# A hybrid SSD decoder block on one Trainium2 core: normalising y inside the SSD steps, and forming block sums of w_down beside the MLP

## The chip, the cores and the metric

The kernel runs on one core of one Trainium2 chip. The metric is the device time of one execution in microseconds; the time of a kernel is the median of its runs. Five engines work in order, each on its own list of instructions: TensorE (PE, with its weight loads shown as PEld), VectorE (DVE), ScalarE (ACT), GpSimd (POOL) and SyncE (SP, which here only issues DMAs; ACT issues some too).

## What is computed

One decoder layer over 1024 positions, width 1024, all in float32, cut to what matters here:

```python
u = rmsnorm(h, norm_mix_w)
gate_a, gate_s, b_a, c_a, v_a, z, xbc, dt_raw = split(u @ w_in)
y_a = (b_a * causal_dwconv3(c_a * v_a)) @ w_a_out
xs, bs, cs = split(silu(causal_dwconv4(xbc) + ssd_conv_b))
y = ssd_chunked_scan(xs, dt, a, bs, cs) + d_skip * xs       # 4 groups, 8 chunks of 128 positions
yf = y * silu(z)                                            # per group of 512 channels:
yf = yf * rsqrt(mean(yf * yf over the group) + 1e-5)        # one factor per position and group
y_s = (yf * ssd_norm_w) @ w_s_out
h = h + (sigmoid(gate_a) * y_a + sigmoid(gate_s) * y_s) @ w_o
v = rmsnorm(h, norm_ffn_w)
h = h + (silu(causal_dwconv3(v @ w_1) + b) * (v @ w_3)) @ w_down
out = rmsnorm(h, final_norm_w)
```

## The kernel before

Every large product is done in three matmuls on a high and a low part of each operand (`split`: ACT casts the high part, DVE or POOL subtracts it to give the low part), 128 rows of weights by 512 positions at a time. Twelve such matmuls, a `product`, are the unit in which the kernel counts: each call of `product` for a `Pair` of output tiles ends in a `tick()`. Pairs of output tiles share sums of blocks (a Strassen-like scheme; the products are named b11, b21, t1 to t4 and b22), so a pair takes seven products.

The stages follow one another on PE. First u is normalised and transposed, then come the projections of w_in with the SSD beside them. The SSD is 32 chunk steps (4 groups, 8 chunks each; `ssd_chunk`), written as a generator with eight parts. The part that runs is set by a table of ticks: step s starts around tick 17 + 6 s, and `STAGES` gives the offset of each part (loading the decay table, loading the chunk, decays, transposes, loading z, the diagonal blocks and the state, squares, norm). Then come the y_a product (`y_a`, two halves of 512 positions), the product with w_s_out (`s_out`, two halves), the product with w_o (`out_proj`), the MLP's 22 up pairs (`ffn_pair`, finished by `ffn_done`), and four sweeps of the down product, which read the block sums of w_down from `td` in device memory and those of the gated activations from `s3d`, `s21d` and `s4d`.

The order on each engine is set by a scheduler that plays the program through with its own durations, and by a few priorities; on the chip each engine then works through its list in that order.

At the end of a chunk step, `zt` holds y * silu(z) for 512 channels (four tiles of 128 channels on the partitions) by 128 positions. Before the change it is squared, summed over the four tiles by DVE into `ss`, and summed over the partitions by a matmul against a column of ones (`pn`, L813). DVE scales that (`yss`, L815), POOL takes the power -1/2 (`yr`, L819, 128 factors on 128 partitions), and `zt` itself is stored without the factor to `yd` (L807, issued by ACT). After four chunks the four columns of factors are transposed by PE (`pr`, L823), copied by ACT (`rr`, L825) and stored to `rd` (L826, SP). In `y_half`, beside `y_a`, each group's 512 factors are loaded back, broadcast to all partitions (`rb`), and DVE multiplies y by the channel's weight and `rb` (L926) before y is split.

The block sums of w_down are formed by `w_sums` (L869): two loads of 128x1024, four subtractions (two on DVE, two on POOL) and four stores to `td`, for each of 11 blocks. They run beside the first `s_out` and the second `y_a`, through `beside(...)`.

Of the kernel before, what the change touches and what calls it, by code (L numbers as in the profile page):

```python
# [8 lines left out]
F32 = mybir.dt.float32  # L9
F32R = mybir.dt.float32r  # L10
AF = mybir.ActivationFunctionType
ALU = mybir.AluOpType
# [41 lines left out]
STAGES = LOAD_M, LOAD_IN, DECAY, TRANS, LOAD_Z, DIAG, SQUARES, NORM = -9, -9, -6, -4, -3, 0, 3, 6  # L54
# [11 lines left out]
def tile_block(  # L66
# [340 lines left out]
    yd, rd = {}, {}  # L407
    for g in range(NG):
        for hf in range(2):
            yd[g, hf] = dram.tile([P, 4, HALF], F32, name=f"yd{g}{hf}")  # L410
            rd[g, hf] = dram.tile([HALF], F32, name=f"rd{g}{hf}")
# [288 lines left out]
    states, decayed, stats = {}, {}, {}  # L700

    def ssd_chunk(s):
# [104 lines left out]
        act.dma_start(yd[g, c // 4][:, :, hts], zt)  # L807
# [6 lines left out]
        rs = tiny(f"yss{nm}")  # L814
        dve.tensor_scalar(rs, pn, 1.0 / HALF, EPS, op0=ALU.mult, op1=ALU.add)  # L815
        if c % 4 == 0:
            stats[g, c // 4] = tiny(f"yr{nm}", 4)
        r = stats[g, c // 4]
        pool.tensor_tensor(r[:, c % 4 : c % 4 + 1], rs, nhalf, op=ALU.pow)  # L819
        if c % 4 == 3:  # L820

            pr = sd_tile(f"pr{nm}")[:4, :P]
            pe.transpose(pr, r, ident)  # L823
            rr = ssp.tile([P, P], F32, tag="ss", name=f"rr{nm}", bufs=1)
            act.copy(rr[:4, :], pr)  # L825
            sp.dma_start(rd[g, c // 4].rearrange("(c p) -> c p", c=4), rr[:4, :])  # L826
# [42 lines left out]
    def w_sums(k):  # L869

        r, r2 = (s4(f"wd{f}{k}")[:, :SEQ] for f in range(2))
        for f, t in enumerate((r, r2)):
            sp.dma_start(t, w_down[f * KF + k])
        b11, b12 = (r[:, h] for h in halves)
        b21, b22 = (r2[:, h] for h in halves)
        sub(b11, b12, b11)
        sub(b12, b22, b12, pool)
        sub(b22, b22, b11)
        sub(b21, b22, b21, pool)
        for i, t in enumerate((b11, b22, b12, b21)):  # L880
            sp.dma_start(td[k, i], t)

# [28 lines left out]
    def y_half(hf, res):  # L911
        for g in range(NG):
            rb = c2(f"rb{hf}{g}")
            sp.dma_start(
                rb,
                rd[g, hf].unsqueeze(0).to_broadcast([P, HALF]),
            )
            hi, lo = big_tile(f"yh{hf}{g}", F32R), big_tile(f"yl{hf}{g}", F32R)
            res.append((hi, lo))
            yt = (extra_tile if hf else big_tile)(f"y{hf}{g}")  # L920
            sp.dma_start(yt, yd[g, hf])
            for j in range(0, 4, 2):
                raw = yt[:, j : j + 2, :]
                for i in range(2):
                    w = wns[:, 4 * g + j + i : 4 * g + j + i + 1]
                    dve.scalar_tensor_tensor(  # L926
                        raw[:, i, :], raw[:, i, :], w, rb, op0=ALU.mult, op1=ALU.mult
                    )
                split(raw, hi[:, j : j + 2, :], lo[:, j : j + 2, :], dve)
                yield  # L930
# [81 lines left out]
    def all_sums():  # L1012
        for k in range(KF):
            w_sums(k)
            yield

# [4 lines left out]
    sums = all_sums()  # L1021
# [5 lines left out]
    mg0 = s_out(0, ys0, beside(ta_half(1, ta1), sums))  # L1027
    yh = y_half(1, ys1)
    y_a(1, ta1, beside(yh, yh, sums))
# [75 lines left out]
    def g_sums(i, cv, free):  # L1105

        a, b = (cv[:, h] for h in halves)
        if i < KF:
            s3 = free[:, :HALF]
            sub(s3, a, b)  # L1110
            sp.dma_start(s3d[i], s3)
            return
# [10 lines left out]
    def ffn_done(i):  # L1123
# [4 lines left out]
        dve.tensor_tensor(cv, cv, h3, op=ALU.mult)  # L1128
        sp.dma_start(gd[i], cv)
        g_sums(i, cv, h3)  # L1130
# [227 lines left out]
```

## Time and profile before

| | |
|---|---|
| median of 3 runs | 1973.02 us (1971.64 to 1974.24) |
| the profiled execution | 1974.46 us |
| its span, first to last instruction | 1972.7 us |
| mean granted TensorE clock | 0.989 |
| busy: PE, DVE, POOL, ACT | 97%, 65%, 63%, 49% |
| projections with the SSD beside them | about 100 to 954 us of the span |
| y_a, s_out and out_proj | about 954 to 1320 us |
| the MLP's up pairs | about 1320 to 1750 us |

A row of the profile names the line, the engine, the operation, the tile written and the tiles read, with numbers left out of the names; a count behind an x says how many instructions a row stands for. The idle time before an instruction is put down to what ended it. PE's busy time is a union of modelled intervals: consecutive matmuls overlap in it, so the distance from one start to the next is the price of a matmul, not the duration printed with it.

### The profile page before, as it was taken

The page shows a single profiled execution, that of the slowest core. Times are in us where ns is not written, and L with a number is a line of the kernel's source. Part 1 is how long each engine was busy: PE and PEld are TensorE (multiplying, and loading weights), DVE is VectorE, ACT ScalarE, POOL GpSimd, SP SyncE. Part 2 cuts the span into 40 slices and gives each one's busy share as a digit, 9 for nine tenths or more (in the row PEclk, how much of TensorE's full clock was granted, in tenths as well). Part 3 has the DMA queues.
Part 4 walks back from the last instruction along what each step waited for, and adds up shares of the span by engine and source line. Part 5 has one row for each costly group of instructions (what it writes and reads, how often), then busy time and mean ns, then how long its engine had stood idle before and what let it go on. Part 6 is the DMA issues. An engine that isn't in the chain of part 4 may idle for free.

```text
span 1972.7 us, 25409 instructions
## 1 busy us (share of the span) xinstructions
PE 1914.5 (97%) x8986; PEld 1572.0 (80%) x8986; DVE 1289.6 (65%) x1429; ACT 962.0 (49%) x1636; POOL 1236.3 (63%) x915
## 2 busy tenths in 40 slices
PE   7899999999999999999999999998999999999998
PEld 6678887787788778888888888876888888878886
DVE  8655567767776777777664833479854655585555
ACT  6345457677546664443542323354344444453334
POOL 6657776866776776676445533458876787845342
PEclk9899999999999999999999999998999999999999
DMA  4133355545445554443998974451323344487653
GB/s 166 54 111 121 122 164 172 162 150 190 155 133 164 164 164 124 146 157 110 382 376 279 356 250 161 161 170 35 136 80 108 101 150 163 139 285 264 206 188 143
DMA packets 180175, 338.42 MB, mean 172 GB/s; under 512 B 15280, under 2 KB 87760, under 8 KB 179024
## 3 DMA queue, kind: packets, MB, share of 16 engines
q1 hardware_dynamic: 93264, 253.95, 37.7%
q10 hardware_dynamic: 86784, 82.85, 13.1%
q8 instruction: 70, 1.15, 0.2%
q14 instruction: 57, 0.47, 0.1%
HBM read 247.34 MB, written 89.41 MB: 171 GB/s over the span
## 4 chain that ended last, share of the span: by engine, by line
PE 80%; DVE 7%; ACT 4%; issue 3%; DMA 3%; POOL 2%; ACTq 1%; SPq 0%; POOLq 0%; DVEq 0%
PE pb11up L268 10%; PE so L268 9%; PE pt1up L268 6%; PE pb11xb L268 5%; PE ya L268 4%; PE pb11cv L268 4%; PE d L1151 3%; PE d L1153 3%; PE d L1152 3%; PE pb11z L268 3%; PE pb21up L268 3%; PE pb11ba L268 2%; PE pt1cv L268 2%; PE pt1xb L268 2%; DMA m<-acd 2%
## 5 line engine op out<-in xcount | busy, mean ns | idle before, releaser
L608 DVE SCALAR_TENSOR_TENSOR cv<-xbc,scw,cv 128x1024 f32<-128x1024 f32 x72 | 122.6, 1704 | 46.3 <-ACT cv L604 45.0
L608 DVE SCALAR_TENSOR_TENSOR h<-fci,fcw,h 128x1024 f32<-128x1024 f32 x44 | 85.9, 1953 | 74.1 <-ACT h L604 73.3
L724 ACT ACTIVATE m<-m,tk 128x128 f32<-128x128 f32 x256 | 79.1, 390 | 95.3 <-DMA m<-acd 91.4
L149 POOL TENSOR_TENSOR l_ws<-raw_ws,h_ws 128x512 fp32r<-128x512 f32 x32 | 46.3, 1447 | 71.1 <-PE so L268 40.8
L148 ACT CAST h_ws<-raw_ws 128x512 fp32r<-128x512 f32 x64 | 39.9, 623 | 96.8 <-PE so L268 69.3
L268 PE MATMUL so<-yh,h_ws 128*128 128x512 f32 x256 | 69.0, 391 | 0.0
L268 PE MATMUL so<-yl,h_ws 128*128 128x512 f32 x256 | 68.6, 389 | 0.0
L268 PE MATMUL so<-yh,l_ws 128*128 128x512 f32 x256 | 68.5, 389 | 0.0
L148 ACT CAST h_wo<-raw_wo 128x512 fp32r<-128x512 f32 x48 | 29.7, 621 | 60.3 <-PE wo L985 32.7
L808 DVE TENSOR_TENSOR eb<-eb 128x256 f32<-128x256 f32 x32 | 28.1, 879 | 45.6 <-ACT eb L806 45.6
L149 DVE TENSOR_TENSOR l_ws<-raw_ws,h_ws 128x512 fp32r<-128x512 f32 x32 | 25.1, 785 | 50.0 <-PE so L268 25.5
L149 POOL TENSOR_TENSOR l_wo<-raw_wo,h_wo 128x512 fp32r<-128x512 f32 x24 | 32.3, 1346 | 39.1 <-PE wo L985 30.7
L268 PEld LDWEIGHTS so<-yh,l_ws 128*128 128x128 f32 x256 | 48.0, 188 | 10.0
L268 PEld LDWEIGHTS so<-yl,h_ws 128*128 128x128 f32 x256 | 48.0, 188 | 10.0
L268 PEld LDWEIGHTS so<-yh,h_ws 128*128 128x128 f32 x256 | 47.8, 188 | 9.7
L1128 DVE TENSOR_TENSOR h<-h 128x1024 f32<-128x1024 f32 x22 | 48.7, 2212 | 9.8 <-ACT h L1127 9.6
L314 DVE TENSOR_TENSOR fci<-fci,pb21up 128x512 f32<-128x512 f32 x18 | 12.4, 688 | 60.3 <-PE pb21up L268 60.3
L149 POOL TENSOR_TENSOR l_t3up<-raw_2up,h_t3up 128x512 fp32r<-128x512 f32 x22 | 30.3, 1376 | 32.7 <-PE pb11up L268 32.7
L984 PE MATMUL wo<-l_wo,mh 128*128 128x512 f32 x128 | 50.0, 391 | 0.0
L983 PE MATMUL wo<-h_wo,mh 128*128 128x512 f32 x128 | 49.9, 391 | 0.0
L985 PE MATMUL wo<-h_wo,ml 128*128 128x512 f32 x128 | 49.7, 391 | 0.0
L1127 ACT ACTIVATE h<-h 128x1024 f32<-128x1024 f32 x22 | 23.4, 1062 | 52.7 <-DVE h L608 52.7
(1125 smaller groups left out, 6571.8 us busy)
## 6 DMA issues: line engine op xcount, KB each, us to landing
m<-acd ACTq DMA_DIRECT2D x32, 512.0 KB, 3.9
raw_ws<-in_w_s_out SPq DMA_DIRECT2D x32, 512.0 KB, 4.7
ssd_in<-cv ACTq DMA_DIRECT2D x24, 512.0 KB, 3.1
in<-ssd_in ACTq DMA_DIRECT2D x32, 384.0 KB, 3.8
raw_wo<-in_w_o SPq DMA_DIRECT2D x24, 512.0 KB, 3.8
wd<-in_w_down SPq DMA_DIRECT2D x22, 512.0 KB, 7.0
td<-wd SPq DMA_DIRECT2D x44, 256.0 KB, 4.3
raw_2up<-in_w_up SPq DMA_DIRECT2D x22, 512.0 KB, 3.4
```

Source lines behind the costliest of these rows:

```text
L148: act.copy(hi, v)
L149: (eng or pool).tensor_tensor(lo, v, f32(hi), op=ALU.subtract)
L268: pe.matmul(ps, wt[:, k, :], ct[:, k, :], start=(start and n == 0), stop=(stop and n == 11), skip_group_check=held,)
L608: dve.scalar_tensor_tensor(cv, ci[:, j : j + SEQ], w[:, j : j + 1], cv, op0=ALU.mult, op1=ALU.add)
L724: act.activation(m[:, h, :], m[:, h, :], AF.Relu, bias=a)
L983: pe.matmul(pss[t], mh, wh, start=k == 0, stop=False)
L984: pe.matmul(pss[t], mh, wl, start=False, stop=False)
L985: pe.matmul(pss[t], ml, wh, start=False, stop=k == NK - 1)
L1128: dve.tensor_tensor(cv, cv, h3, op=ALU.mult)
L1151: pe.matmul(ps, aa[0][:, ts], bb[0], start=k == 0, stop=False)
L1152: pe.matmul(ps, aa[0][:, ts], bb[1], start=False, stop=False)
L1153: pe.matmul(ps, aa[1][:, ts], bb[0], start=False, stop=k == KF - 1)
```

## The change

Two things are moved. First, the factor of each chunk is applied to `zt` inside its own SSD step, before it is stored. POOL's power gives 128 factors on 128 partitions; DVE multiplies the identity by them into the tile of the sums, and a matmul of the 128x128 matrix of ones with that diagonal matrix puts the same 128 factors, along the positions, on every partition (`pr`). DVE then does the four multiplications by weight and factor (a `scalar_tensor_tensor` of 128x128 each, with `pr` read from PSUM) and ACT issues the store of the scaled `zt`. This is a ninth part of the step, SCALE, two ticks behind NORM; NORM moves from tick 6 to 5 and the load of z from -3 to -2. The transposes, the copies, the `rd` stores, the `rb` loads and the 32 multiplications in `y_half` go.

Second, `w_sums` is called from `g_sums`, for each of the MLP's first 11 pairs, once that pair's gated product is issued. Its two tiles are those of `side` (two buffers), and all four subtractions are DVE's.

```diff
-STAGES = LOAD_M, LOAD_IN, DECAY, TRANS, LOAD_Z, DIAG, SQUARES, NORM = -9, -9, -6, -4, -3, 0, 3, 6
+STAGES = LOAD_M, LOAD_IN, DECAY, TRANS, LOAD_Z, DIAG, SQUARES, NORM, SCALE = -9, -9, -6, -4, -2, 0, 3, 5, 7
...
         act.activation(sq, zt.rearrange("p j l -> p (j l)"), AF.Square)
-        act.dma_start(yd[g, c // 4][:, :, hts], zt)
...
         pe.matmul(pn, sums, ones[:, :1], start=True, stop=True)
-        rs = tiny(f"yss{nm}")
-        dve.tensor_scalar(rs, pn, 1.0 / HALF, EPS, op0=ALU.mult, op1=ALU.add)
-        if c % 4 == 0:
-            stats[g, c // 4] = tiny(f"yr{nm}", 4)
-        r = stats[g, c // 4]
-        pool.tensor_tensor(r[:, c % 4 : c % 4 + 1], rs, nhalf, op=ALU.pow)
-        if c % 4 == 3:
-
-            pr = sd_tile(f"pr{nm}")[:4, :P]
-            pe.transpose(pr, r, ident)
-            rr = ssp.tile([P, P], F32, tag="ss", name=f"rr{nm}", bufs=1)
-            act.copy(rr[:4, :], pr)
-            sp.dma_start(rd[g, c // 4].rearrange("(c p) -> c p", c=4), rr[:4, :])
+        r = tiny(f"yr{nm}")
+        dve.tensor_scalar(r, pn, 1.0 / HALF, EPS, op0=ALU.mult, op1=ALU.add)
+        pool.tensor_tensor(r, r, nhalf, op=ALU.pow)
+
+        dve.tensor_scalar(sums, ident, r, None, op0=ALU.mult)
+        yield
+        pr = sd_tile(f"pr{nm}")[:, :P]
+        pe.matmul(pr, ones, sums, start=True, stop=True)
+        for j in range(4):
+            w = wns[:, 4 * g + j : 4 * g + j + 1]
+            dve.scalar_tensor_tensor(zt[:, j, :], zt[:, j, :], w, pr, op0=ALU.mult, op1=ALU.mult)
+        act.dma_start(yd[g, c // 4][:, :, hts], zt)
...
     def y_half(hf, res):
-            rb = c2(f"rb{hf}{g}")
-            sp.dma_start(
-                rb,
-                rd[g, hf].unsqueeze(0).to_broadcast([P, HALF]),
-            )
...
-                for i in range(2):
-                    w = wns[:, 4 * g + j + i : 4 * g + j + i + 1]
-                    dve.scalar_tensor_tensor(
-                        raw[:, i, :], raw[:, i, :], w, rb, op0=ALU.mult, op1=ALU.mult
-                    )
                 split(raw, hi[:, j : j + 2, :], lo[:, j : j + 2, :], dve)
...
-    mg0 = s_out(0, ys0, beside(ta_half(1, ta1), sums))
+    mg0 = s_out(0, ys0, beside(ta_half(1, ta1)))
-    y_a(1, ta1, beside(yh, yh, sums))
+    y_a(1, ta1, beside(yh, yh))
...
+    def w_sums(k):
+
+        r, r2 = (side(f"wd{f}{k}", w_down[f * KF + k]) for f in range(2))
+        b11, b12 = (r[:, h] for h in halves)
+        b21, b22 = (r2[:, h] for h in halves)
+        sub(b11, b12, b11)
+        sub(b12, b22, b12)
+        sub(b22, b22, b11)
+        sub(b21, b22, b21)
+        for i, t in enumerate((b11, b22, b12, b21)):
+            sp.dma_start(td[k, i], t)
+
+    def g_sums(i, cv, free, after):
         a, b = (cv[:, h] for h in halves)
         if i < KF:
+            with tc.issue_after(after.ins):
+                w_sums(i)
             s3 = free[:, :HALF]
...
-        dve.tensor_tensor(cv, cv, h3, op=ALU.mult)
+        gated_ = dve.tensor_tensor(cv, cv, h3, op=ALU.mult)
         sp.dma_start(gd[i], cv)
-        g_sums(i, cv, h3)
+        g_sums(i, cv, h3, gated_)
```

The scheduler lays the new work into the engines' lists. In the rows below the number at the end of a tile's name only tells instances apart; `zt_2` is chunk 2 of its group.

DVE in the SSD stage, third group, chunks 2 and 3, before: the scaling of the sums (L815) stands between a pair's addition and the next chunk's diagonal.

```order
L810 TENSOR_TENSOR ss_2_5847<-eb_2_5652 128x128
L363 TENSOR_TENSOR z_5566<-u2z_5662,pt1z_5711 128x512
L815 TENSOR_SCALAR yss_2_5919<-pn_2_5917 128x1
L784 TENSOR_TENSOR in_3_5659<-in_3_5659,pd_3_5922 128x512
L786 TENSOR_TENSOR eb_3_5849<-po_3_5931,eb_3_5849 128x512
L787 TENSOR_TENSOR in_3_5659<-in_3_5659,eb_3_5849 128x512
L793 TENSOR_TENSOR st_5362<-sn_2_5753,pst_3_5936 128x512
L803 TENSOR_TENSOR zt_3_5852<-in_3_5659,zt_3_5852 128x512
```

The same place now: the product with the identity (L816) stands three instructions behind the scaling of the sums, and the four multiplications by `pr` (L822) behind the next chunk's `zt`.

```order
L813 TENSOR_SCALAR yr_2_5994<-pn_2_5992 128x1
L363 TENSOR_TENSOR z_5645<-u2z_5742,pt1z_5802 128x512
L149 TENSOR_TENSOR l_b22xb_6248<-raw_2xb_5946,h_b22xb_6247 128x512
L783 TENSOR_TENSOR in_3_5739<-in_3_5739,pd_3_6015 128x512
L816 TENSOR_SCALAR ss_2_5939<-ident,yr_2_5994 128x128
L785 TENSOR_TENSOR eb_3_5969<-po_3_6024,eb_3_5969 128x512
L786 TENSOR_TENSOR in_3_5739<-in_3_5739,eb_3_5969 128x512
L792 TENSOR_TENSOR st_5435<-sn_2_5839,pst_3_6029 128x512
L802 TENSOR_TENSOR zt_3_5972<-in_3_5739,zt_3_5972 128x512
L149 TENSOR_TENSOR l_t1g_6287<-raw_1g_6116,h_t1g_6286 128x512
L822 SCALAR_TENSOR_TENSOR zt_2_5762<-zt_2_5762,wns,pr_2_6069 128x128 x4
```

So L816, which needs POOL's power, now has the next chunk's L785 to L802 queued behind it.

PE at the same place, before: the sums over the partitions (`pn`) and then only the next chunk's matmuls and products.

```order
L813 MATMUL pn_2_5917<-ones,ss_2_5847 128x1
L770 MATMUL pd_3_5922<-m_3_5657,xd_3_5816 64x128 x8
L777 MATMUL po_3_5931<-in_3_5659,st_5362 128x128 x4
L783 MATMUL pst_3_5936<-xe_3_5818,bk_3_5821 128x512
L268 MATMUL pt1xb_5959<-us1h,h_t1xb_5960 128x512 x4
L268 MATMUL pt1xb_5959<-us1l,h_t1xb_5960 128x512 x4
L268 MATMUL pt1xb_5959<-us1h,l_t1xb_5961 128x512 x4
```

Now, behind `pn` and some two products:

```order
L268 MATMUL pt1xb_6052<-us1h,l_t1xb_6054 128x512 x3
L268 MATMUL pb11xb_5883<-us3h,h_t3xb_6077 128x512 x4
L268 MATMUL pb11xb_5883<-us3l,h_t3xb_6077 128x512 x4
L268 MATMUL pb11xb_5883<-us3h,l_t3xb_6078 128x512 x4
L268 MATMUL pb11g_6118<-ua11h,h_b11g_6119 128x512 x2
L819 MATMUL pr_2_6069<-ss_2_5939,ones 128x128
L729 MATMUL px_4_6093<-ident,in_4_5943 128x128 x4
```

A matmul that needs the power now follows `pn` in every chunk, 32 in all, where 8 transposes stood.

SP in the MLP, around one pair, before: the loads of two weight tiles, and two stores.

```order
L158 DMA raw_1up_12652<-in_w_up 128x1024
L1129 DMA gd<-h_12221 128x1024
L158 DMA raw_2up_12691<-in_w_up 128x1024
L1111 DMA s3d<-h_12221 128x512
L158 DMA raw_1up_12796<-in_w_up 128x1024
```

Now, from one pair's first weight tile to the next pair's:

```order
L158 DMA raw_1up_12712<-in_w_up 128x1024
L1110 DMA gd<-h_12245 128x1024
L1082 DMA td<-wd_12504 128x512
L158 DMA raw_2up_12751<-in_w_up 128x1024
L1092 DMA s3d<-h_12245 128x512
L1082 DMA td<-wd_12504 128x512
L1082 DMA td<-wd_12506 128x512 x2
L1069 DMA wd_12660<-in_w_down 128x1024
L1069 DMA wd_12662<-in_w_down 128x1024
L158 DMA raw_1up_12868<-in_w_up 128x1024
```

Each of the first 11 pairs has six more DMAs in SP's list, four of which wait for DVE, ahead of the next pair's first weight tile.

More of the change, by code (lines that the diff above doesn't have):

```diff
@@ L406, in tile_block @@
     acd = dram.tile([2, P, P], F32, name="acd")
-    yd, rd = {}, {}
+    yd = {}
     for g in range(NG):
@@ L410, in tile_block @@
             yd[g, hf] = dram.tile([P, 4, HALF], F32, name=f"yd{g}{hf}")
-            rd[g, hf] = dram.tile([HALF], F32, name=f"rd{g}{hf}")
     ead = dram.tile([2, P, P], F32, name="ead")
@@ L698, in tiles @@
         return t.rearrange("p (j l) -> p j l", j=4)
-    states, decayed, stats = {}, {}, {}
+    states, decayed = {}, {}
     def ssd_chunk(s):
@@ L867, in add @@
         eng.tensor_tensor(o, p, q, op=ALU.add)
[L869 to L881, printed above, removed]
     def ta_half(hf, res):
@@ L1010, in v_norm @@
         return v
[L1012 to L1015, printed above, removed]
     def beside(*gens):
         return lambda j: [next(g, None) for g in gens]
-    sums = all_sums()
     ta0, ta1, ys0, ys1 = [], [], [], []
@@ L1103, in side @@
         return t
-    def g_sums(i, cv, free):
+    def w_sums(k):
[9 more added lines that the diff above has]
+    def g_sums(i, cv, free, after):
         a, b = (cv[:, h] for h in halves)
         if i < KF:
+            with tc.issue_after(after.ins):
+                w_sums(i)
             s3 = free[:, :HALF]
```

## Prediction

> **What bounds the kernel now.** First the page's busy times and its chain of waits, then the engines by stretches (span, PE busy, PEld, DVE, ACT, POOL, granted clock, DMA share, GB/s).
>
> ```profile
> PE 1914.5 (97%) x8986; PEld 1572.0 (80%) x8986; DVE 1289.6 (65%) x1429; ACT 962.0 (49%) x1636; POOL 1236.3 (63%) x915
> PE 80%; DVE 7%; ACT 4%; issue 3%; DMA 3%; POOL 2%; ACTq 1%; SPq 0%; POOLq 0%; DVEq 0%
> ...
> 250.00:850.00 600.00, 587.59 (x3057) 478.62 (x3056) 442.89 (x523) 363.34 (x678) 422.86 (x322) 1.00 0.50 158
> 930.00:1000.00 70.00, 70.00 (x311) 57.81 (x310) 48.77 (x54) 32.67 (x47) 33.58 (x22) 1.00 0.95 361
> 1000.00:1100.00 100.00, 100.00 (x442) 82.68 (x441) 59.35 (x68) 35.07 (x53) 48.16 (x34) 1.00 0.90 319
> 1380.00:1400.00 20.00, 20.00 (x90) 16.41 (x89) 16.91 (x15) 7.23 (x12) 18.76 (x14) 1.00 0.53 175
> 1400.00:1420.00 20.00, 20.00 (x90) 16.57 (x89) 17.75 (x15) 8.15 (x13) 17.84 (x13) 1.00 0.22 76
> 1420.00:1500.00 80.00, 80.00 (x355) 66.24 (x354) 44.21 (x41) 35.63 (x56) 56.03 (x43) 1.00 0.31 101
> ```
>
> PE is the bound nearly everywhere: 58.2 us of the span (1972.7 - 1914.5) are all the time in which it has nothing to do. In the SSD stretch it idles 12.4 us of 600. From 930 to 1100, where the change takes work away, it idles not at all, although the DMA engines there are 90 to 95% busy. That "busy" could hide a slower cadence, so I read the cadence, from the chain in order of time (start, length, what) in that stretch and from PE's timeline in the MLP, where DMA is light; between them stands DVE's scaling of y by `rb` (ns least, median and most; first and last start).
>
> ```profile
> 1003.12 87.04 PE so L268 x384
> ...
> L926 DVE SCALAR_TENSOR_TENSOR y<-y,wns,rb x32: 737/745/1781, 966.8 to 1114.4; 128x512 f32<-128x512 f32 x32
> ...
> 1436.25 1.07 PE L268 MATMUL pt1up<-vs4h,l_b22up 128*128 128x512 f32 x4
> 1437.15 1.07 PE L268 MATMUL pt1up<-vs1h,h_t1up 128*128 128x512 f32 x4
> ```
>
> 87.04 / 384 = 227 ns a matmul, and (1437.15 - 1436.25) / 4 = 225 ns. The crowded stretch runs no slower. So whatever DVE, POOL, SP and the DMA engines get rid of between 930 and 1160 is worth nothing: the 32 multiplications of y by `rb` (median 745 ns), the 8 `rb` loads, and the 44 subtractions and 66 transfers of `w_sums`. What the change adds to PE, and every wait it makes for PE, does count.
>
> **PE's own work.** The timeline around two places of the SSD stage gives prices as distances between starts.
>
> ```profile
> 425.63 0.27 PE L732 MATMUL pb<-ident,in 128*128 128x128 f32 x1
> 425.74 0.39 PE L734 MATMUL pc<-in 128*128 128x128 f32 x2
> 425.88 1.17 PE L268 MATMUL pt1xb<-us1h,h_t1xb 128*128 128x512 f32 x4
> 426.89 1.08 PE L268 MATMUL pt1xb<-us1l,h_t1xb 128*128 128x512 f32 x4
> ...
> 436.88 0.28 PE L813 MATMUL pn<-ones,ss 128*128 128x1 f32 x2
> 437.02 1.18 PE L268 MATMUL pb11xb<-ua22h,h_t4xb 128*128 128x512 f32 x4
> 438.04 1.08 PE L268 MATMUL pb11xb<-ua22l,h_t4xb 128*128 128x512 f32 x4
> ...
> 937.51 0.27 PE L823 MATMUL pr<-ident,yr 128*4 128x128 f32 x1
> 937.53 1.17 PE L268 MATMUL pb21g<-ua12h,h_b21g 128*128 128x512 f32 x4
> 938.54 1.08 PE L268 MATMUL pb21g<-ua12l,h_b21g 128*128 128x512 f32 x4
> ```
>
> Four product matmuls take 0.91 us from start to start. `pc`, a float32 matmul of 128x128 by 128 columns like the new `pr`, has two records; from its start to the second group after it are 1.15 us, so it costs 0.24 us. `pn` comes to 0.25 by the same step, the transpose of the old `pr` to 0.12. New: 32 x 0.24 = 7.7 us. Gone: 8 x 0.12 = 1.0. Net +6.7 us, bounded below by 32 x 2 x 0.11 - 1.0 = 6.0 (each record priced as `pb`, 425.74 - 425.63) and above by 32 x 0.25 - 1.0 = 7.0. The Trainium skill's page "TensorE: Matmul & The Clock Gate" (Back-to-back issue gap) gives about 81 ns for a sustained matmul of 128 columns: two of these would make `pr` 0.16 us, 5.2 us in all, and an estimate of +4.2 net. Its 131 ns for 512 columns is not what this trace shows (225 ns), so I keep the rows' price.
>
> **Waits for the factor.** Before, the power was waited for by one transpose in four chunks. PE's waits, POOL's wait for DVE, and the slowest and the quickest of the 32 chunks (timeline):
>
> ```profile
> PE pr L823 <- POOL yr L819: 2.8, 3, 2.3
> POOL yr L819 <- DVE yss L815: 14.7, 8, 4.5
> ...
> 662.63 0.28 PE L813 MATMUL pn<-ones,ss 128*128 128x1 f32 x2
> 663.44 0.15 DVE L815 TENSOR_SCALAR yss<-pn 128x1 f32<-128x1 f32 x1
> 671.72 1.48 POOL L149 TENSOR_TENSOR l_t2g<-t2g,h_t2g 128x512 fp32r<-128x512 f32 x1
> 673.16 0.59 POOL L819 TENSOR_TENSOR yr<-yss,nhalf 128x1 f32<-128x1 f32 x1
> ...
> 751.36 0.28 PE L813 MATMUL pn<-ones,ss 128*128 128x1 f32 x2
> 752.00 0.55 POOL L819 TENSOR_TENSOR yr<-yss,nhalf 128x1 f32<-128x1 f32 x1
> ```
>
> POOL waited for DVE in only 8 chunks; in the other 24 POOL was the late one. From `pn`'s start to the power's end are 1.2 us at best and 11.1 at worst. The new `pr` stands about two products behind `pn` on PE, some 6.4 to 12.6 us of matmuls at the prices above, mostly 7.5 to 9.7. Set against each chunk's own delay, plus 0.35 us for DVE's multiplication of the identity, six chunks come late, three by 1.7 to 1.9 us, the others by less, 6.6 us in all. The 2.8 us of old waits go. The new ones could be 0 (POOL's list is new too) or 11.2 (all 32 wait the 0.35 us that the old eight averaged); I take 6.6.
>
> **DVE and ACT in the SSD stage.** DVE gets four multiplications and the identity's per chunk. The nearest row is a 128x128 operation that reads PSUM:
>
> ```profile
> L751 DVE TENSOR_TENSOR cb<-pc,tri 128x128 f32<-128x128 f32 x32 | 8.9, 278 | 0.0
> ACT m L724 <- DMA m<-acd: 84.9, 23, 6.9
> ```
>
> 5 x 0.28 = 1.4 us a chunk, 45 us in all. DVE goes from 443 busy of 600 to about 482. The worse part is that the identity's multiplication holds DVE's list until POOL is done: directly behind L813 in 13 chunks, one to three instructions later in the rest. Taking each chunk's old delay from DVE's scaling to the end of the power, less what stands between, I get about 80 us of standing, on top of 482 in 600; it largely replaces idle time. Queued behind it are the next chunk's `eb`, `st` and `zt`. Who waits for these: POOL's `sn`, ACT's squares, and PE through PSUM banks. The pairs are covered, as two rows of a product's low part and its use show for the MLP, and as I find for the SSD's pairs too (mostly 10 to 20 us):
>
> ```profile
> 1423.29 0.68 DVE L149 TENSOR_TENSOR l_b22up<-raw_2up,h_b22up 128x512 fp32r<-128x512 f32 x1
> ```
>
> It ends at 1423.97 and PE reads it at 1436.25, 12.3 us later. ACT's list now holds the `yd` store until DVE has scaled, and the copies that free PE's accumulators (u2, u3) stand behind it; ACT already loses 84.9 us there to the loads of `m`. For all of this I take +2 us. The ends are -12.4 (all of PE's idle time there vanishes by the new order) and +20 (a quarter of the 80 us reaches PE); I stay near zero because the rows show long leads.
>
> **The MLP.** 11 pairs get four subtractions on DVE. Their rows, and the transfers (KB each, us to landing):
>
> ```profile
> L864 DVE TENSOR_TENSOR wd<-wd x11: 678/693/1779, 931.6 to 1150.6; 128x512 f32<-128x512 f32 x11
> L864 POOL TENSOR_TENSOR wd<-wd,wd x11: 1284/1292/2379, 940.3 to 1153.7; 128x512 f32<-128x512 f32 x11
> td<-wd SPq DMA_DIRECT2D x44, 256.0 KB, 4.3
> wd<-in_w_down SPq DMA_DIRECT2D x22, 512.0 KB, 7.0
> ```
>
> 4 x 0.69 = 2.8 us a pair against 8.5 us of DVE idle time per pair of 19.1 us (7 products of 12 matmuls) from 1420 on (35.8 in 80): hidden, by idle DVE. The first four pairs are different, with shorter turns and DVE 85 to 89% busy from 1380 to 1420: 11 us of subtractions into 5.3 us of idle time. Pair 1's first subtraction also waits for a load that waits for pair 0's last store, 4.3 + 7.0 us by rows taken under crowded DMA. So DVE runs some 6 to 10 us late there, within the 12 us lead. On SP the next weights stand behind stores that wait for DVE, with about a pair's lead (19 us). I take +1; the ends are 0 and +10 (the lead is gone at the start).
>
> **The sum.** 6.7 - 2.8 + 6.6 + 2 + 1 = +13.5 us. The profiled execution took 1974.46 us, 1.8 beyond its span and 1.4 above the median of 1973.02. It would take 1988.0; from the median I forecast 1986.5 us. By the page's price for `pr` alone it would be 1984.0.
>
> **Rivals.**
> 1. POOL is not late in the new order and everything else is covered: +6.7 - 2.8 = +3.9, 1976.9 us, just at the edge of what a measurement of this kernel tells from no change (0.2%, 3.9 us). For it: 19 of the 32 old delays are under 5.5 us. Against it: POOL's list still has the same eight operations ahead of the late power at 662. If in addition PE's other idle time shrinks a little, the result is "same".
> 2. DVE's standing behind POOL becomes a bound: 482 + 75 of 600 us leave little to catch up; a quarter reaching PE is +20, with the work 1998 us or more. For it: the next chunk's state stands behind it. Against it: leads of 10 to 20 us.
> 3. Faster: the new order removes PE's stalls in the SSD stage. They are 12.4 us in 250 to 850; some end on ACT copies held up behind loads of `m`, and ACT loses the `rr` copies. All of it gone gives 6.7 - 12.4 = -5.7 us, 1967.3; it decides only if more than 10.6 of the 12.4 us go and no new wait comes. Nothing in the lists moves those loads of `m` by more than a few places.
> 4. The first MLP pairs lose their lead: +10 instead of +1, 1995.5 us.
>
> **How the numbers follow.** Forecast (1980 to 1992) 45%, rival 1 with its neighbours (1970 to 1980) 23%, rival 2 17%, rival 4 9%, rival 3 6%. The range 1976 to 2002 leaves out rival 3, part of rival 1 and the tail of rival 2, about 20%. Faster by over 0.2% is rival 3, 0.06. Within 0.2% is rival 1's lower half, 0.13. Slower is the rest, 0.81.
>
> **What would show it.** In the changed profile: 64 records of `pr` at 0.24 us of cadence; PE waits on `pr` or, behind it, on DVE of about 7 us; PE's idle time from 250 to 850 above 12.4 us; DVE's idle time before the identity's multiplication put down to POOL `yr`, tens of us; the same 87 us for 384 `so` matmuls; and no PE waits after 1420. I am wrong if PE's idle time in the SSD stage falls, or if `pr` costs 0.1 us, or if the down sweeps find block sums late.

## The result, and the profile after

The changed kernel takes 2000.16 us (median of 4 runs, 1995.87 to 2001.43) against 1973.51 us for the kernel before on the same chip (1971.64 to 1974.24): a ratio of 1.0133, interval [1.0115, 1.015], so +26.65 us. The forecast was +13.5. The profiled execution of the changed kernel is the quickest of its four; its span is 1994.1 us, 21.4 above that of before. What makes the others some 5 us longer stays open, since only this one was profiled. In the medians of the experiments below two executions are left out that took far longer than the others of their kernel: one of 6841 us where DVE's scaling is left out too (with it that median is +11.6, as two expectations have it), and one of 2145 us with the old places of `pn` and z.

First, from the page of the changed kernel, the busy times and the chain of waits by engine; then some of PE's longest waits (what it was about to do, the releaser, us in total, times, longest).

```profile
PE 1926.5 (97%) x9042; PEld 1570.5 (79%) x9042; DVE 1328.1 (67%) x1579; ACT 958.8 (48%) x1626; POOL 1199.2 (60%) x893
PE 72%; DVE 10%; issue 6%; POOL 5%; ACT 4%; DMA 2%; ACTq 0%; SPq 0%; POOLq 0%; DVEq 0%
...
PE pt1up L268 <- DVE vs1l L149: 4.9, 1, 4.9
PE pr L819 <- DVE ss L816: 4.9, 5, 1.3
...
PE pt3up L268 <- DVE fci L333: 3.3, 2, 2.9
```

`pt1up` waited 3.9 us in the kernel before too, and `pr` 2.8; `pt3up` did not wait there. PE gained 12 us of busy time and the chain of waits lost 8 points on PE, which went to DVE, POOL and issue. Where the 21.4 us are is told by four stretches of each kernel, cut at the first SSD product, the first `ya`, the first `pb11up` and the first `d` matmul (start and end, length, then busy time of PE, PEld, DVE, ACT and POOL, as in the prediction). Before:

```profile
101.60:954.00 852.40, 834.35 (x4204) 680.27 (x4203) 602.81 (x694) 484.21 (x887) 592.13 (x447) 1.00 0.47 151
954.00:1314.55 360.55, 360.55 (x1609) 297.80 (x1608) 197.36 (x246) 137.42 (x228) 161.77 (x115) 1.00 0.76 270
1314.55:1744.51 429.96, 419.09 (x1829) 345.91 (x1828) 273.92 (x250) 190.09 (x299) 329.62 (x235) 0.98 0.37 121
1744.51:1972.73 228.22, 218.67 (x961) 179.76 (x959) 141.75 (x142) 96.55 (x124) 89.10 (x62) 0.99 0.63 212
```

After:

```profile
101.23:966.40 865.17, 844.68 (x4249) 679.36 (x4247) 634.52 (x853) 482.35 (x878) 584.88 (x447) 1.00 0.46 147
966.40:1329.68 363.28, 363.28 (x1621) 300.04 (x1620) 148.71 (x192) 136.58 (x228) 125.47 (x93) 1.00 0.60 205
1329.68:1766.90 437.22, 421.74 (x1829) 346.24 (x1828) 324.60 (x295) 190.62 (x300) 337.34 (x235) 0.98 0.50 171
1766.90:1994.14 227.24, 218.41 (x961) 179.83 (x959) 145.02 (x142) 95.47 (x123) 87.98 (x61) 0.99 0.63 212
```

The SSD stretch grew by 12.8 us, the second by 2.7, the MLP by 7.3, and the last shrank by 1.0. The second holds 12 more PE records: one SSD product of 12 matmuls now falls behind the first `ya` and costs its 2.7 us there, so it belongs to the SSD part, 15.5 us in all. Apart from it that stretch is as long as before, although DVE lost 49 us of work in it, POOL 36 and the DMA engines a fifth of their share; PE is busy all the time in both. The relief there was worth nothing.

Three rows explain more than the waits of PE. They are DVE's groups in the changed kernel (busy time, mean ns of one; idle time just before, and what ended it):

```profile
L816 DVE TENSOR_SCALAR ss<-ident,yr 128x128 f32<-128x128 f32 x32 | 27.3, 852 | 54.1 <-POOL yr L814 52.3 <-POOL fci L1024 1.7
L861 DVE TENSOR_TENSOR wd<-wd,wd 128x512 f32<-128x512 f32 x22 | 27.4, 1245 | 0.0
...
L861 DVE TENSOR_TENSOR wd<-wd 128x512 f32<-128x512 f32 x22 | 27.1, 1230 | 0.1
```

DVE stands 54 us ahead of the identity's multiplication (idle, with the rest of its list held behind it; 52.3 of them are put down to POOL's power), and the multiplication itself takes 0.85 us in the mean, not the 0.28 that I took. The timeline shows why, at two chunks (start, us, engine, what):

```profile
425.55 0.55 POOL L814 TENSOR_TENSOR yr<-yr,nhalf 128x1 f32<-128x1 f32 x1
...
426.07 1.26 POOL L326 TENSOR_TENSOR raw_1z<-raw_1z,t2z 128x512 f32<-128x512 f32 x1
426.14 1.28 DVE L816 TENSOR_SCALAR ss<-ident,yr 128x128 f32<-128x128 f32 x1 [4.57 <-POOL yr L814]
...
427.47 0.49 PE L819 MATMUL pr<-ss,ones 128*128 128x128 f32 x2 [1.25 <-DVE ss L816]
...
481.71 0.55 POOL L814 TENSOR_TENSOR yr<-yr,nhalf 128x1 f32<-128x1 f32 x1 [1.47 <-DVE yr L813]
482.29 0.29 DVE L816 TENSOR_SCALAR ss<-ident,yr 128x128 f32<-128x128 f32 x1 [0.66 <-POOL yr L814]
```

At 481.71 POOL has nothing to do next and the multiplication takes 0.29 us. At 426.07 POOL goes on to its next operation, 0.07 us ahead of DVE; DVE's operation then ends with POOL's, 1.28 us after its start. The power's end releases both engines at the same moment, so this is no chance: in 18 of the 32 chunks the multiplication takes 1.26 to 1.31 us, in the other 14 it takes 0.28 or 0.29. The block sums meet POOL in the same way: they take 0.68 us where POOL is idle and up to 1.78 where it is not, 54.5 us for 44. The Trainium skill's page "SBUF — State Buffer" (Who interferes with whom) says that DVE's second port pair is shared with GpSimd and held for a whole instruction, and that a `tensor_scalar` in a two-port mode and a `tensor_tensor` with both inputs in SBUF contend for it. The rows agree, with +1.0 and +1.1 us; whether this multiplication runs in such a mode, no row shows.

### The profile page after: what moved, and what is told of

It is laid out like the page before. It is cut to its first block, busy times and chain, and to the rows that moved or that the text cites. A ratio compares the mean times of both kernels' runs of the same rounds, so it can differ in the third digit from the quotient of the medians.

```text
span 1994.1 us, 25568 instructions
## 1 busy us (share of the span) xinstructions
PE 1926.5 (97%) x9042; PEld 1570.5 (79%) x9042; DVE 1328.1 (67%) x1579; ACT 958.8 (48%) x1626; POOL 1199.2 (60%) x893
## 4 chain that ended last, share of the span: by engine, by line
PE 72%; DVE 10%; issue 6%; POOL 5%; ACT 4%; DMA 2%; ACTq 0%; SPq 0%; POOLq 0%; DVEq 0%
PE pb11up L268 9%; PE so L268 9%; PE pt1up L268 5%; PE ya L268 4%; PE pb11xb L268 4%; PE d L1132 3%; PE d L1133 3%; PE d L1134 3%; PE pb11z L268 3%; PE pb11cv L268 3%; PE pb21up L268 2%; PE pt1xb L268 2%; PE pb11g L268 2%; PE pt1z L268 2%; PE pb11ba L268 2%
## 5 line engine op out<-in xcount | busy, mean ns | idle before, releaser
L797 POOL TENSOR_TENSOR sn<-st,cdb 128x512 f32<-128x512 f32 x24 | 36.4, 1516 | 47.1 <-DVE st L792 43.6
L816 DVE TENSOR_SCALAR ss<-ident,yr 128x128 f32<-128x128 f32 x32 | 27.3, 852 | 54.1 <-POOL yr L814 52.3
L149 POOL TENSOR_TENSOR l_wa<-raw_wa,h_wa 128x512 fp32r<-128x512 f32 x16 | 22.5, 1406 | 60.1 <-PE ya L268 26.8
L149 DVE TENSOR_TENSOR l_wo<-raw_wo,h_wo 128x512 fp32r<-128x512 f32 x24 | 20.8, 869 | 54.4 <-ACT h_wo L148 26.8
L268 PEld LDWEIGHTS so<-yl,h_ws 128*128 128x128 f32 x256 | 48.0, 188 | 10.1
L268 PEld LDWEIGHTS so<-yh,l_ws 128*128 128x128 f32 x256 | 48.1, 188 | 10.1
L751 DVE TENSOR_TENSOR m<-m,cb 128x1024 f32<-128x1024 f32 x32 | 52.0, 1624 | 0.5
```

What stands on the lines that cost most here:

```text
L149: (eng or pool).tensor_tensor(lo, v, f32(hi), op=ALU.subtract)
L268: pe.matmul(ps, wt[:, k, :], ct[:, k, :], start=(start and n == 0), stop=(stop and n == 11), skip_group_check=held,)
L751: dve.tensor_tensor(m, m, cb.unsqueeze(1).to_broadcast([P, HG, P]), op=ALU.mult)
```

## The experiments

Times are medians; "+" is the difference to the median of the kernel before in the same comparison (1972.27 to 1974.12 us), and the brackets are the ratio's 95% interval times that median.

**The two halves alone.** The SSD part alone keeps the block sums beside y_a and s_out; the sums alone keep the SSD stage as before (their diffs are the two halves of the change).

> The SSD part of the change alone (factor spread by TensorE, y scaled beside the SSD's steps); block sums of w_down where they were before, beside y_a and s_out. My theory: of the +26.6 us, about 15 arise ahead of s_out: 7.4 us are PE's own work on pr (32 x 0.26 - 1.0), the rest are products and pr itself that come late because DVE's list is held up (by POOL's power, and by POOL's next operation after it). So +14 to +16, 1988 us. Rival A (only the new work on PE costs, the rest of the 26.6 us comes from the block sums and from the spread between executions): +7 to +9, 1981 us. Rival B (the two parts need each other: the sums beside s_out take DVE time that the y part frees): below +5.

> The block sums of w_down alone moved beside the MLP's first pairs, all four subtractions on DVE; the SSD stage as before. My theory: DVE is full in the first four pairs, the forecast's lead of 12 us is used up there, and PE waits: +6 to +8.5, 1980 to 1982 us, with PE waits between 1320 and 1420 as in the changed kernel (two waits behind 1390 of 3 us and of some tenths), and a half-speed clock spell after the longest. Rival (the sums cost what I forecast, +1, and the MLP's loss in the changed kernel is a consequence of the SSD part): 1973 to 1975 us.

The SSD part alone: 1991.26 us, +19.0 [17.4, 22.5]. The sums alone: 1980.87 us, +8.6 [5.3, 11.0]. Together 27.6 against the measured 26.65, so the halves add. The stretches of the SSD stage and the MLP, of the SSD part alone and of the sums alone:

```profile
100.92:971.51 870.59, 847.83 (x4261) 681.68 (x4260) 636.89 (x855) 482.83 (x879) 585.77 (x447) 1.00 0.46 148
1332.07:1762.07 430.00, 418.73 (x1830) 345.67 (x1829) 274.53 (x251) 190.75 (x299) 330.05 (x235) 0.98 0.36 122
```

```profile
102.46:952.02 849.56, 831.69 (x4193) 678.01 (x4191) 597.41 (x693) 484.51 (x888) 590.47 (x447) 1.00 0.47 150
1315.29:1752.11 436.82, 422.03 (x1829) 346.46 (x1828) 325.54 (x294) 189.77 (x299) 338.51 (x235) 0.98 0.50 170
```

Each half lengthens its own stretch only: the MLP is 430.0 with the SSD part and 436.8 with the sums. The SSD part cost more than the 14 to 16 us that I expected. The SSD stage is 849.6 us in the sums' kernel and 852.4 before, with hardly a change in its lists: single profiled executions differ by that much.

**The sums four pairs later.**

```diff
-        if i < KF:
-            with tc.issue_after(after.ins):
-                w_sums(i)
+        if 4 <= i < KF + 4:
+            with tc.issue_after(after.ins):
+                w_sums(i - 4)
+        if i < KF:
```

> The changed kernel with each block sum formed four pairs later (pairs 4 to 14 instead of 0 to 10), where DVE idles 30% and more. My theory: the MLP's loss of 7.3 us sits in the first four pairs alone, so 5 to 8 us come back: 1992 to 1995 us, and the waits on pt3up and pt1up behind 1390 are gone. Rival (what costs is the traffic of the sums' loads and stores on SP's queue, or PE simply does more): no change, 1999 to 2001 us.

1995.74 us, +23.5 [20.3, 26.6]: 3.2 us less than the change's +26.65, with intervals that overlap. The trace is clearer than the times. The MLP's stretch:

```profile
1330.06:1760.86 430.80, 419.98 (x1829) 345.96 (x1828) 328.92 (x293) 187.40 (x298) 342.34 (x234) 0.98 0.50 172
```

It is 6.4 us shorter, with more DVE work in it (328.9 us) than in the changed kernel, and the waits on `pt3up` are gone. The sums' loads and stores are all still there. So the MLP's loss sits in the first four pairs.

**Half of the sums on POOL.**

```diff
-        sub(b12, b22, b12)
+        sub(b12, b22, b12, pool)
         sub(b22, b22, b11)
-        sub(b21, b22, b21)
+        sub(b21, b22, b21, pool)
```

> The block sums alone moved into the MLP (+8.6 us, 1980.9 us), but two of the four subtractions of each pair on POOL, as they were before the change. If DVE being full in the first four pairs is what costs: half or more comes back, 1974 to 1978 us. Rival (what costs is that the sums' loads and stores stand in SP's queue, or that any work there delays the lot): 1979 to 1983 us. Rival (POOL is as full there as DVE, and the late one is now POOL): 1981 to 1986 us with PE waiting for POOL.

1983.47 us, +10.3 [8.5, 13.6]: nothing is won over the sums alone. In the first four pairs (length, PE, PEld, DVE, ACT, POOL) neither DVE nor POOL has much room, least of all in the first of these rows:

```profile
1380.00:1400.00 20.00, 16.67 (x71) 12.87 (x71) 19.47 (x15) 5.61 (x8) 18.76 (x13) 1.00 0.60 218
1400.00:1420.00 20.00, 19.08 (x85) 15.39 (x84) 17.22 (x16) 6.62 (x10) 15.18 (x11) 1.00 0.53 167
1420.00:1440.00 20.00, 17.67 (x78) 14.32 (x77) 14.84 (x11) 8.41 (x14) 16.81 (x11) 1.00 0.58 205
```

The POOL rival fits in part: POOL was 94% busy in the first of these before anything was put there (prediction, 1380 to 1400), and one of the two DVE subtractions now meets it in every pair (ns least, median, most):

```profile
L864 DVE TENSOR_TENSOR wd<-wd x11: 1772/1777/1783, 1381.6 to 1570.0; 128x512 f32<-128x512 f32 x11
```

But none of PE's waits there is put down to POOL, as that rival said: `pt1up` waits 2.6 us for DVE's `u2up`, and `pb11up` 2.3 for ACT's.

**The identity's multiplication on POOL.**

```diff
-        dve.tensor_scalar(sums, ident, r, None, op0=ALU.mult)
+        pool.tensor_scalar(sums, ident, r, None, op0=ALU.mult)
```

> The changed kernel with the identity's multiplication by the factor on POOL, right behind the power, instead of on DVE. My theory: DVE stands 52 us behind the power, and 17 of its 32 multiplications begin just as POOL begins its next operation and then take 1.28 us instead of 0.29; on POOL both are gone, and the five waits of PE for pr (4.9 us) and the late items behind DVE (pn, pst, pb21cv) shrink: 3 to 6 us back, 1994 to 1997 us. Rival (PE's work alone costs): 1999 to 2001. Rival (POOL is the engine that is behind; one more operation of 0.6 to 1.3 us a chunk there delays it further): slower than the changed kernel, 2002 to 2006 us.

1996.49 us, +24.2 [21.5, 28.0], 2.4 less than the change with overlapping intervals: unclear. Its SSD stretch is 867.0 us, no shorter than the 865.2 of the changed kernel. PE's waits moved: `PE pr` now waits 13.5 us for POOL, and those on `pn`, `pst` and `pb21cv` are gone.

**The SSD part taken apart.** Four kernels leave out one thing more each, all made from the SSD part alone (+19.0).

With `pr` a product of constants, y is scaled by 1, and nothing waits for the factor but DVE's list:

```diff
-        pe.matmul(pr, ones, sums, start=True, stop=True)
+        pe.matmul(pr, ones, ident, start=True, stop=True)
```

> The SSD part alone, but pr is the product of ones with the bare identity: y is scaled by 1 instead of the factor, and neither PE nor DVE's scaling waits for the factor; power and identity multiplication stay, and DVE still stands behind the power. The SSD part alone took 1991.3 us (+19.0), PE waiting there 5.8 us for pr. Theory W (work and waits): the waits for pr go, 5 to 8 us back, 1983 to 1986 us. Rival P (nearly all of the +19 is PE doing more, and a wait removed at pr returns at the next late product): 1989 to 1992 us. Rival D (what costs is DVE standing behind the power, not PE's wait for pr): 1989 to 1992 us here, and it comes back only with the next kernel.

1995.46 us, +21.3 [18.4, 23.9]. My theory missed: PE's waits for `pr` are gone and the time is not less. In the SSD part alone they were

```profile
PE pr L819 <- DVE ss L816: 5.8, 6, 1.3
```

Taking them away won nothing in sum; but some 65 of the 857 instructions of DVE's list in this stage stand in another place here, so what they are worth by themselves is not shown.

Then the multiplication's factor is a constant too, so both instructions stay and DVE no longer stands behind POOL:

```diff
-        dve.tensor_scalar(sums, ident, r, None, op0=ALU.mult)
+        dve.tensor_scalar(sums, ident, ones[:, :1], None, op0=ALU.mult)
```

> As the kernel with the constant pr (1995.5 us, +21.3): POOL still computes the power and DVE still multiplies the identity, but by a column of ones, so DVE does not stand behind POOL. Without both instructions it took 1985.2 us. If the standing is what these 10.3 us are: 1984 to 1988 us. Rival (POOL's and DVE's own time for them is): 1992 to 1996 us.

1988.49 us, +14.6 [12.8, 18.0], 6.7 below the last one, with intervals that do not overlap. In the kernel with the constant `pr` DVE's row was

```profile
DVE ss L816 <- POOL yr L814: 39.4, 27, 3.0
```

and here it is absent. The two SSD stretches:

```profile
101.59:974.98 873.39, 850.58 (x4261) 684.38 (x4259) 633.57 (x855) 482.06 (x878) 589.29 (x447) 0.99 0.46 148
```

```profile
101.61:967.30 865.69, 847.44 (x4260) 684.74 (x4259) 644.66 (x854) 482.04 (x878) 587.60 (x447) 0.99 0.46 149
```

DVE is busier (644.7 against 633.6) in a stretch that is 7.7 us shorter: DVE's standing behind POOL costs, not its load. The two lists differ in little else. Apart from the 32 multiplications, which now run 0.7 to 9.2 us ahead of the power's end, DVE's instructions of this stage stand in the same order, and PE's too but for one or two. Nor is it the meeting with POOL: the multiplication takes 0.71 us in the mean here and took 0.76 with the wait.

Next, power and multiplication are left out:

```diff
-        pool.tensor_tensor(r, r, nhalf, op=ALU.pow)
-        dve.tensor_scalar(sums, ident, ones[:, :1], None, op0=ALU.mult)
```

> As the kernel with the constant pr, and the power on POOL and the identity's multiplication on DVE are left out as well (y is scaled by 1), so that DVE never stands behind POOL for the factor. What is left of the change is pn and pr on PE and five operations of 0.34 us or less on DVE. Theory W: only PE's 32 x 0.26 - 1.0 = 7.4 us less the old waits of 2.8 remain, and perhaps 2 for DVE's scaling: 1977 to 1980 us. Rival D: equal to W here, but 8 to 12 us below the kernel with the constant pr. Rival P (PE's work is dearer than its cadence shows): 1984 us or more.

1985.15 us, +11.0 [8.5, 13.4]: 3.6 us for the instructions themselves, intervals just overlapping.

Last, DVE's four multiplications by `pr` go, and the store of y stands where it was before:

> As the kernel without power and identity multiplication (1985.2 us, +11.0), and DVE's four multiplications of y by the factor are left out too (y stays unnormalised), with the store of y where it was before. What is left is the changed table of stages, and pr on PE two ticks behind pn. In the kernel before, the same 32 matmuls right behind pn cost 1.9 us. If the rest of the +11.0 is DVE's scaling and the store that waits for it: 1975 to 1979 us. Rival (pn and pr each break the stream of products at a place of their own, and PE's own work is the rest): 1982 to 1986 us.

1983.66 us, +10.5 [8.1, 13.8]. The scaling, 128 operations of 0.34 us, and the store behind it cost nothing that these runs can tell, and without factor and scaling more than half of the +19 is still there.

**The store of y two ticks later,** on ACT's list, by another stage behind SCALE:

> The SSD part alone, with the store of y issued on ACT's queue two ticks after the scaling instead of right behind it, so that ACT does not stand behind PE's pr and DVE's scaling. The kernel before with a store on ACT's queue that waits for the power took 2013.6 us, +39.5 from eight such places, so ACT's list is dear to hold. If ACT's standing is a good part of the +19: 3 to 8 us back, 1983 to 1988 us. Rival (DVE's standing alone counts): 1990 to 1992 us.

1990.85 us, +17.7 [15.2, 21.1]: no difference, in line with that. All else stands in the same order.

**What is left: PE's work, its place, and the table.** On the kernel before, one extra matmul per chunk like `pr`, which nothing reads: right behind `pn`, and then two ticks later, where the change has `pr`.

```diff
+        pq = sd_tile(f"pq{nm}")[:, :P]
+        pe.matmul(pq, ones, ident, start=True, stop=True)
```

> The kernel before, with one more matmul per chunk, ones times identity (128x128 by 128 columns, float32, two records, as pr), right behind pn, which nothing reads and which waits for nothing new. Prices PE's work by itself. By the cadence in the trace (0.26 us each, 32 of them): +8.3 us, 1980.6 us. Rival (such a matmul is dearer than the step to the second group after it shows, since it breaks the stream of products): +12 to +16, 1984 to 1988 us. Rival (part of it falls into PE's 18 us of idle time in the SSD stage): +4 to +6.

> The kernel before with 32 extra matmuls as pr (ones times identity, nothing reads them), now not right behind pn at tick 6 (which cost 1.9 us) but two ticks later, where the change has pr. Settles what is left of the +11.6 of the kernel without factor and scaling beside the table (+3.9) and the matmuls (+1.9). If the place of pr makes it: +6 to +9, 1980 to 1983 us. Rival (the place does not matter, the parts do not simply add): +1 to +4, 1975 to 1978 us.

Behind `pn`: 1976.05 us, +1.9 [0.4, 3.8], far below all I expected. Two ticks later: 1978.18 us, +5.7 [3.9, 7.3], between what the two theories gave. The SSD stretches of the two:

```profile
102.57:956.54 853.97, 840.88 (x4269) 686.92 (x4267) 591.45 (x695) 482.21 (x886) 585.83 (x447) 1.00 0.48 151
```

```profile
101.09:959.18 858.09, 842.41 (x4269) 687.58 (x4267) 598.28 (x695) 482.13 (x886) 592.15 (x447) 1.00 0.47 151
```

PE is busy 6.5 and 8.1 us longer than before, so the matmuls do cost their time on PE. But its idle time falls from 18.05 us (852.40 - 834.35) to 13.09 and 15.68. My reading is that PE waits there for moments set by other engines, and that work of its own ahead of such a moment only shortens the wait; more of it is absorbed behind `pn` than two ticks later. The lists leave another: the scheduler laid some 50 and 80 of DVE's 710 instructions of this stage in another place in these two kernels, and some 60 in the next one, the edit's own among them. What that costs was not tried apart.

The table of stages alone, on the kernel before:

```diff
-STAGES = ..., LOAD_Z, DIAG, SQUARES, NORM = -9, -9, -6, -4, -3, 0, 3, 6
+STAGES = ..., LOAD_Z, DIAG, SQUARES, NORM = -9, -9, -6, -4, -2, 0, 3, 5
```

> The kernel before with two numbers of the changed table alone: pn and power at tick 5 instead of 6, the load of z at -2 instead of -3. No new work. The kernel that has the changed table, pr, and neither factor nor scaling took +11.6 us, while the same pr right behind pn in the old table took +1.9. If the table makes the difference: +6 to +10 here, 1979 to 1983 us. Rival (the place of pr, two ticks behind pn, makes it): 1971 to 1975 us.

1977.78 us, +3.9 [2.0, 5.7]: half of what the theory said, yet not nothing. 5.7 + 3.9 = 9.6, against +10.5 for the kernel that has both: it adds up within the intervals. The SSD part with the old places of `pn` and z, and `pr` at 8:

> The SSD part alone (1991.3 us, +19.0) with pn and power back at tick 6, the load of z back at -3, and pr with the scaling at 8, two ticks behind as in the change. Same work. If the table costs: 6 to 10 us back, 1981 to 1985 us. Rival (the work and the standing behind POOL cost, wherever pn is): 1989 to 1993 us.

1989.91 us, +16.1 [13.6, 20.5]; the 2.9 us to the SSD part alone are within the intervals. With the standing in it, the table's share cannot be seen.

**Two tries to end DVE's standing by the table,** with the identity's multiplication two and three ticks behind the power:

> The SSD part alone (1991.3 us, +19.0), with the identity's multiplication issued two ticks after the power instead of right behind it (stages 5: pn and power, 7: identity, 8: pr, scaling and store), so that DVE finds the power done. Same work on every engine. If DVE standing behind the power is what costs (leaving power and multiplication out gave 10.3 us): 8 to 11 us back, 1980 to 1984 us, and DVE's 53 us of idle time before the multiplication falls to a few. Rival (the power and the multiplication cost by their own time on POOL and DVE, not by the standing): 1988 to 1992 us. Rival (pr later by a stage makes the store and the loads of z late): above 1992.

> The SSD part alone (1991.3 us) with the identity's multiplication three ticks behind the power (stages 5, 8, 9). Two ticks behind, DVE still stood 46.9 us for the power and nothing was won (1994.6 us); with the same two instructions and no wait between them, 6.7 us came back. If DVE's standing falls below 20 us here and standing is what costs: 4 to 7 us back, 1984 to 1988 us. Rival (POOL is still the late one): standing above 35 us and 1990 to 1996 us. Rival (the standing falls and the time does not): below 20 us of standing and 1990 us or more.

1994.61 us, +21.5 [18.2, 24.9], and 2012.73 us, +40.2 [35.9, 43.6]. DVE stands 46.9 and 52.2 us for the power, as before. The trace shows that the multiplication still runs 0.03 to 0.04 us behind the power in nearly every chunk: the number in the table did not move it behind enough other work. What moved is `pr`, the scaling and the store. These two kernels don't tell what the standing costs; that rests on the pair above. Nor was it found why the second is so much slower: its SSD stage takes 894.6 us, against 870.6 in the SSD part alone.

**The kernel before without its transposes of the factors,** stored straight in elements of 4 bytes, on ACT's queue and then on SP's:

```diff
-            pr = sd_tile(f"pr{nm}")[:4, :P]
-            pe.transpose(pr, r, ident)
...
-            sp.dma_start(rd[g, c // 4].rearrange("(c p) -> c p", c=4), rr[:4, :])
+            act.dma_start(rd[g, c // 4].rearrange("(c p) -> p c", c=4), r)
```

> The kernel before without its eight transposes of the factors: the four columns of factors are stored to HBM straight from where POOL writes them, on ACT's queue in elements of 4 bytes. Nothing of PE waits for the power. By the rows: 8 x 0.12 us of work and 2.8 us of waits go, -3.8 us, 1968.5 us. Rival (the waits return at the next late product, or the store in small elements holds ACT's list): 1971 to 1975 us.

> The kernel before without its transposes of the factors, as the one that took 2013.6 us, but with the store of the factors on SP's queue, so that ACT's list is not held by the power. If ACT's standing was the cost: below 1975 us, by the forecast's rows -3.8, 1969 us. Rival (the store's 512 elements of 4 bytes delay the other transfers): 1985 us or more. Rival (SP's queue, which carries the weights, is now the one held): 1978 to 1990 us.

2013.63 us, +39.5 [36.1, 41.7], and 2009.37 us, +35.5 [29.2, 39.7]. So it is not ACT's list that is held: either queue costs about the same. It was meant to beat both kernels. None of the versions tried beats the kernel before.

## Why the prediction was right or wrong

The sum came out 13 us short. The SSD part alone cost 19.0 where 6.7 - 2.8 + 6.6 + 2 = 12.5 had been counted, and the block sums 8.6 where 1 had been. The terms that failed are the two that were taken as nearly covered, DVE's standing and the first MLP pairs, and one that was put at nothing, the table of stages. Of the signs named, PE's idle time from 250 to 850 did rise, from 12.4 to 14.4 us.

**y_a to w_o worth nothing: right.** `so`'s 384 matmuls take as long as before, in the chain of the changed kernel:

```profile
1018.24 87.04 PE so L268 x384
```

**PE's own work, +6.7: right as a price, wrong as a cost.** The SSD stretch's busy time confirms 0.20 to 0.25 us each (6.5 and 8.1 us for 32). Added to the span they are 1.9 us behind `pn` and 5.7 in the place of `pr`, where 7.7 had been counted. The step that failed is "What the change adds to PE, and every wait it makes for PE, does count": 18 us of idle time in 852 were enough to take up part of the work. This error made the forecast too high, not too low.

**Waits for the factor, +6.6 - 2.8: right in the trace, wrong as a term.** PE waits 4.9 us for `pr` in the changed kernel, 5.8 in the SSD part alone. The constant `pr` took them away and won nothing in sum. So a PE wait in this stage can't be added as a term; it may only be the place where the delay of another engine shows.

**DVE and ACT in the SSD stage, +2: mis-sized.** DVE's standing behind the power was foreseen as about 80 us, it was 54, and "largely replaces idle time" was the step that failed: standing costs 6.7 us (for the 39 us of it in the kernel with the constant `pr`), and the two instructions about 3.6, with intervals that just overlap. That is rival 2's mechanism, at a third of its +20. ACT's held store, which I named, costs nothing that the runs can tell. The 0.28 us for the identity's multiplication came from a row that reads PSUM; this one reads SBUF, met POOL in 18 of 32 chunks, and took 0.85 in the mean.

**The table of stages: missed.** I priced neither `pn` a tick earlier nor z loaded a tick later, and put them at nothing without a reason; together they cost 3.9 us by themselves.

**The MLP, +1: mis-sized, +8.6.** The step that failed is "within the 12 us lead": in the first pair the late DVE reached PE. I multiplied 0.69 us, a median, where the groups of the kernel before already give means of 0.94 and 1.18 us for the same DVE line:

```profile
L864 DVE TENSOR_TENSOR wd<-wd,wd 128x512 f32<-128x512 f32 x11 | 13.0, 1178 | 17.2 <-POOL wd L864 15.7 <-DMA raw_wa<-in_w_a_out 1.5
L864 DVE TENSOR_TENSOR wd<-wd 128x512 f32<-128x512 f32 x11 | 10.3, 939 | 14.2 <-DMA wd<-in_w_down 14.2
```

With 1.24 us each, four are 5.0 a pair. The stretch was misread too: the 40 us from 1380 to 1420 hold the sums of little more than two pairs, not of four. In the changed kernel, 15 us later, nine subtractions begin there, 13.1 us of work for the 5.3 us that DVE had idle, and its two rows are nearly full:

```profile
1395.00:1415.00 20.00, 17.05 (x68) 13.62 (x68) 19.22 (x17) 6.58 (x10) 15.02 (x12) 0.91 0.57 210
1415.00:1435.00 20.00, 19.18 (x83) 15.06 (x83) 18.55 (x18) 6.71 (x10) 14.94 (x11) 1.00 0.56 198
```

The 12 us of lead, measured in a pair behind 1420, did not hold there. From the changed kernel's timeline:

```profile
1397.98 1.78 DVE L861 TENSOR_TENSOR wd<-wd 128x512 f32<-128x512 f32 x1
...
1403.09 2.48 DVE L861 TENSOR_TENSOR wd<-wd,wd 128x512 f32<-128x512 f32 x2
1405.49 0.68 DVE L333 TENSOR_TENSOR fci<-u3up,pt4up 128x512 f32<-128x512 f32 x1
...
1406.32 1.71 PE L268 MATMUL pt3up<-vs3h,h_t3up 128*128 128x512 f32 x4 [2.95 <-DVE fci L333]
```

`fci`, which reads `pt4up` out of PSUM and which PE waits for ahead of `pt3up`, stands in DVE's list behind three subtractions, two of them stretched to 1.75 and 1.78 us. PE waits 2.95 us and its next four matmuls take 1.7 us where 1.07 is usual: the trace has the granted clock at 0.5 from 1406.7 to 1410.1, and at 1.0 before and after. That is rival 4, which I gave 9%. That later pairs hide the sums was right, nearly: beyond 1420 three waits of 0.4 to 0.5 us are left.

**The ledger.** Table 3.9 and `pr` in its place 5.7, both together 10.5; DVE's scaling 0.5; the two instructions of the factor 3.6; standing 6.7; PE's wait for the real factor -2.3. The scaling and the negative one are no more than the spread. In sum 19.0, by construction of the steps; with the sums' 8.6 it is 27.6, against 26.65. So standing and the sums have a shown cause. For the 10.5 us of table and `pr` the kernels show that they cost; what holds PE back there was not found.

## What to carry to other kernels

Price an instruction from the mean of a row with the same operands and neighbours: a DVE operation that POOL's operation releases meets POOL's next one whenever POOL has one ready, here in 18 of 32 chunks. A wait of the bound engine is not a term of a sum until a kernel without it is faster; as far as they were found, the costs here were in an engine that stood with its list held, and in a stretch where three engines were full already. Before work is moved "beside" something, add it up for the few turns in which the engines are fullest, not for the mean of the stage.

## What the runs showed of the hardware

A store of 2 KB in 512 elements of 4 bytes delays the large loads beside it. In the kernel with these stores on ACT's queue they take 10.1 us to land (median of 8; the trace has no landing for the stores in rows of the kernel before). A load of `m` (512 KB) takes 4.4 us there (median of 32); the four that were issued within 1.5 us of such a store took 8.3, 9.4, 10.0 and 13.6. In the changed kernel, which has no such stores, none but the first two of the 32 takes over 6.5. ACT waits for `m`, and PE for ACT's copies, up to 7 us at a time:

```profile
PE pb11xb L268 <- ACT u2xb L331: 9.6, 3, 7.0
PE pb11g L268 <- ACT u3g L331: 9.6, 2, 5.3
PE pb11g L268 <- ACT u2g L331: 5.6, 1, 5.6
```

The eight stores cost 35 to 40 us, on either queue. That they do it through the late loads is read from the trace and was not tried apart.
